# Three more panels of each channel mixer multiply a second pair of weight chunks with seven products

## The chip, the cores and the metric

The kernel runs on one core of one Trainium2 chip. The metric is the device time of a run in microseconds (us). Before the change it is 2210.26 us, the median of three runs (2210.10, 2210.26 and 2210.79). One more execution was taken by the hardware profiler; all views of the profile belong to it.

## The reference, cut to what matters

The model is a decoder trunk of two layers over 256 tokens of width 2048. Each layer has a mixer (gated linear attention in the first, forgetting attention in the second, both beside a cross-attention on 256 memory tokens) and then a channel mixer of hidden width 5632:

```
def conv_ffn(h, w_up, conv_w, conv_b, w_down):
    u = causal_dwconv(h @ w_up, conv_w, conv_b)
    a, val = split_cols(u, [FFN_HIDDEN, FFN_HIDDEN])
    return (jax.nn.silu(a) * val) @ w_down
```

The change touches only `h @ w_up`, a product of 256 x 2048 with 2048 x 11264 numbers, once in each layer. All data are 32-bit floats.

## The kernel before, in words

**Split numbers.** Each operand of a matrix product is split in a high part that TensorE takes as `fp32r` and a low part, the rest. One product of two split numbers is three matmuls: high by high, low by high, high by low. The weights come from memory in units of 128 partitions x 1024 numbers into a ring of five buffers `raw` (`split_unit`, load at L224). ScalarE (ACT in the profile) writes the high part `whi` (L234), VectorE (DVE) subtracts and writes the low part `wlo` (L235). `whi` and `wlo` are rings of five buffers each, so splitting can run at most a few units ahead of TensorE (PE). Both steps are scheduled with a raised priority (`AHEAD`).

**A panel.** `h @ w_up` is cut in eleven panels (`up_pair(j)`, j = 0, 4, ..., 40; panel number j // 4). A panel has 1024 columns, half for `a` and half for `val`, and its 2048 rows are 16 units, one for each chunk of 128 rows. The 256 tokens are two blocks and the columns two halves, so a unit needs four block products, each of three matmuls of 128 x 128 by 128 x 512: twelve matmuls.

**Seven products.** `pair_steps` can treat two neighbouring chunks together as a 2 x 2 block product, with seven products in place of eight (Strassen's scheme in Winograd's form): 21 matmuls instead of 24. It needs sums of the token blocks of the two chunks, made once for a layer (`input_sums`, into `usum`), and sums of the weights, made for each panel. So for a pair the weights go into two buffers `raw2` (L432, a ring of two; the loads are issued after the last load already issued), the raw values of three blocks are split as they are (L383, L384, first 512 columns and then 1024), four subtractions of 512 columns on VectorE form the sums in place (L438 to L441), and the two buffers are split once more (1024 columns each). The third split on ScalarE is issued after the last of these subtractions. The products p1, p5, p7 and p6 collect over all pairs of a panel in one set of four accumulators and p2, p3, p4 and x collect in the other; the two sets change places from panel to panel. After the last pair `early` combines the first set (L1503 to L1510); at the end of the panel `late` adds the second (L1514) and a transpose follows (L1465).

**Which panels.** Every panel takes the pair of chunks 6 and 7 that way (`SEVEN_UP`). Panels whose number stands in `MORE_IN` take chunks 11 and 12 as well (`SEVEN_MORE`). A panel with one pair runs six single units, the pair, and eight single units. A panel with two pairs runs the first pair after four single units, then three single units, the second pair, and five more. The `usum` of the second pair is made during the first panel, at its step 13 (L1524).

**What follows a panel.** Its two halves leave through GpSimd's (POOL's) DMA queue to DRAM and back, turned (L651, L656), and then need on ScalarE twelve scaled copies each (L1415) and an activation (L1428), and on VectorE two additions (L1422), one product (L1435) and a split (L529, L530). For four of the halves of a layer VectorE also makes token sums for the down projection (L477 to L480, L688, L689). These steps are put between the units of the next panels by `tick`: a step is let go 7 or 8 units after the panel's end, and each unit adds a credit of 1.45 (1.7 in panels with two pairs; none for a pair) that the steps use up; the two halves of a panel cost 20.4 together.

**Order in a layer.** Panels 0 to 4; two down projections of 16 units over the first 16 hidden chunks; panels 5 to 7; two of 12 units; panels 8 to 10; and the last four column groups of the down projection, which begin with a wide one that has a pair of its own. Each engine runs its instructions in one fixed order, made when the kernel is built, and loads of weights run in order on one queue (SP's).

Of the kernel before, what the change touches and what calls it, by code (L numbers as in the profile page):

```python
# [34 lines left out]
SEVEN_UP = (6,)  # L35
SEVEN_DOWN = {4: 0, 10: 1, 20: 0, 34: 1}
SEVEN_MORE = 11
MORE_IN = (2, 5, 6, 8, 9)
SCRATCH = 4096


# [106 lines left out]
def _trunk(ctx: ExitStack, tc: tile.TileContext, xt, xtok, memt, wp, wgu, gns, gfin, cnv, par, msk, out):  # L148
# [1246 lines left out]
    def ffn(l, nx, h, m, ys, zs, landing, then, pool, temps, last=None, spare=None):  # L1395
        with tc.tile_pool(name=f"ffn{l}", bufs=1) as fp:
# [60 lines left out]
            def turn(j, wait):  # L1457

                count[0] += 1
                slot = count[0] % 2  # L1460
                y, z = ys[slot], zs[slot]

                def evac(b, a):
                    with tc.high_priority(offset=AHEAD):
                        turned_last[0] = V.transpose(y[:, :, :, b, :], a.rearrange("p (k c i) -> p c k i", c=4, i=32))  # L1465
                    if b:
                        away = far_away(dram, flat(y), T, nc.gpsimd)
                        back = lambda: away(flat(z))
                        steps = [(0.5, lambda s=s, c=c, i=i: tap_of(j, s, c, i, slot)) for n in ((1, 2), (0,))
                                 for s in range(2) for c in range(2) for i in n]  # L1470
                        steps += [(1.0, lambda: add_tap(1)), (1.0, lambda: add_tap(2)), (0.5, silu),
                                  (1.0, lambda: gated(j, 0)), (0.7, lambda: gated(j, 1))]
                        returns.append((clock[0] + 3, slot, back, [(clock[0] + wait, *step) for step in steps]))

                return evac
# [18 lines left out]
            def up_pair(j):  # L1494

                count[2] += 1
                second = j // 4 in MORE_IN
                turns = [turn(j + 2 * h_, 7 if not h_ and j // 4 + 1 in MORE_IN else 8) for h_ in range(2)]
                u = {}

                def early(bank):
                    u.update({(b, h_): temps(2 * b + h_) for b in range(2) for h_ in range(2)})
                    S.activation(u[0, 1], bank["p1"], AF.Copy)  # L1503
                    S.activation(u[0, 0], bank["p1"], AF.Copy, scale=scale(0))
                    V.tensor_tensor(u[0, 1], bank["p6"], u[0, 1], ALU.add)
                    V.tensor_tensor(u[1, 0], bank["p7"], u[0, 1], ALU.add)
                    V.tensor_tensor(u[0, 1], bank["p5"], u[0, 1], ALU.add)
                    V.tensor_tensor(u[1, 1], bank["p5"], u[1, 0], ALU.add)
                    for b, h_ in ((0, 1), (1, 0), (1, 1)):
                        S.activation(u[b, h_], u[b, h_], AF.Copy, scale=scale(b))  # L1510

                def late(b, h_, a):
                    with tc.issue_after(turned_last[0].ins) if h_ and not b else nullcontext():
                        V.scalar_tensor_tensor(u[b, h_], a, scale(b), u[b, h_], ALU.mult, ALU.add)  # L1514
                    turns[h_](b, u[b, h_])

                return pair_steps(where["up", l, j], h, {k: up_sums[k] for k in (*SEVEN_UP, SEVEN_MORE)[: 1 + second]},
                                  count[2] % 2, pool, early, late, 2 * second)
# [8 lines left out]
            def drive(steps, share=1.45):  # L1527
                for k in steps:
                    tick(share if k >= 0 else 0.0)

            def drive_up(j):
                drive(up_pair(j), 1.7 if j // 4 in MORE_IN else 1.45)

# [266 lines left out]
```

## Time and profile before

| what | value |
|---|---|
| median of three runs | 2210.26 us |
| the profiled execution's own time | 2211.01 us |
| its span in the profile | 2209.2 us |
| PE busy | 2197.2 us, 10303 matmuls |
| DVE busy | 1804.7 us |
| ACT busy | 1426.7 us |
| first channel mixer, panels 0 to 10 | from 457 us to 1075 us of the span |
| second channel mixer, panels 0 to 10 | from 1494 us to 2113 us |

In the views, PE is TensorE, a name such as L413 is the line of the kernel at which the instruction was issued, and `x144` counts instructions. `acc`, `ps_o`, `ps_s` and `ps_t` are accumulators. `fvt` and `temp` are buffers for what a panel leaves, and `raw` stands for both `raw` and `raw2`, since instructions are named by the program's names without their numbers.

### The profile page before, as it was taken

How to read it: one execution, taken by the hardware profiler on the slowest of the kernel's cores; microseconds unless marked ns; L12 is line 12 of the kernel's file. 1: busy time of each engine (PE TensorE's matmuls, PEld its weight loads, DVE VectorE, ACT ScalarE, POOL GpSimd, SP SyncE). 2: the span in 40 equal slices, each digit the busy share in tenths (PEclk: the TensorE clock that was granted, in tenths of full speed). 3: DMA queues.
4: the chain of work that ended last, by engine and by line, in shares of the span. 5: the costliest groups of instructions: out<-in, count | busy, mean ns of one | idle time of the engine just before them, and what ended most of it. 6: DMA issues, size and time to landing. Idle time of an engine off the chain costs nothing.

```text
span 2209.2 us, 30105 instructions
## 1 busy us (share of the span) xinstructions
PE 2197.2 (99%) x10303; PEld 1849.1 (84%) x10303; DVE 1804.7 (82%) x2679; ACT 1426.7 (65%) x2268; POOL 137.2 (6%) x257
## 2 busy tenths in 40 slices
PE   9999999999999999999999999999999999999998
PEld 7888888888888888888888998888888888888886
DVE  7768976688998888889877669668898888888996
ACT  6655655556787568657865555455788657765774
POOL 0000000001100010001110000000100000100010
PEclk9999999999999999999999999999999999999999
DMA  9777677867778567666778767776677757676673
GB/s 367 253 223 220 192 209 225 256 219 249 235 248 267 189 212 248 229 232 221 247 252 259 227 201 244 228 240 231 227 239 236 254 184 247 228 266 206 223 271 131
DMA packets 166291, 515.42 MB, mean 233 GB/s; under 512 B 20780, under 2 KB 42552, under 8 KB 166136
## 3 DMA queue, kind: packets, MB, share of 16 engines
q1 hardware_dynamic: 149064, 460.99, 63.1%
q0 software_dynamic: 16496, 51.71, 7.4%
q8 instruction: 81, 1.33, 0.2%
q10 hardware_dynamic: 576, 0.79, 0.1%
q14 instruction: 74, 0.61, 0.1%
HBM read 469.62 MB, written 43.79 MB: 232 GB/s over the span
## 4 chain that ended last, share of the span: by engine, by line
PE 99%; DVE 0%; ACT 0%; issue 0%; DVEq 0%; ACTq 0%
PE acc L413 29%; PE acc L339 26%; PE ps_s L413 15%; PE ps_o L413 8%; PE ps_t L413 7%; PE acc L310 3%; PE acc L265 3%; PE ps_s L339 2%; PE acc L369 2%; PE acc L263 1%; PE ps_s L1036 0%; PE ps_o L702 0%; PE ps_s L702 0%; PE ps_s L1309 0%; PE ps_s L1082 0%; PE ps_o L1264 0%
## 5 line engine op out<-in xcount | busy, mean ns | idle before, releaser
L235 DVE TENSOR_TENSOR wlo<-raw,whi 128x1024 fp32r<-128x1024 f32 (+2 forms) x697 | 828.0, 1201 | 235.3 <-ACT whi L234 214.4
L234 ACT ACTIVATE whi<-raw 128x1024 fp32r<-128x1024 f32 (+2 forms) x697 | 717.6, 1046 | 356.1 <-PE acc L339 135.2
L339 PE MATMUL acc<-whi,B 128*128 128x512 f32 (+3 forms) x1248 | 290.9, 369 | 0.0
L383 ACT ACTIVATE whi<-raw 128x1024 fp32r<-128x1024 f32 (+1 forms) x160 | 151.9, 954 | 197.1 <-DVE raw L439 64.5
L339 PEld LDWEIGHTS acc<-whi,B 128*128 128x128 f32 x1248 | 226.8, 188 | 28.1
L384 DVE TENSOR_TENSOR wlo<-raw,whi 128x1024 fp32r<-128x1024 f32 (+1 forms) x160 | 173.4, 1085 | 25.9 <-ACT whi L383 23.5
L413 PE MATMUL acc<-whi,mix 128*128 128x512 f32 x750 | 191.9, 389 | 0.0
L413 PE MATMUL acc<-whi,B 128*128 128x512 f32 x728 | 188.4, 389 | 0.0
L413 PEld LDWEIGHTS acc<-whi,mix 128*128 128x128 f32 x750 | 140.8, 188 | 29.3
L413 PEld LDWEIGHTS acc<-whi,B 128*128 128x128 f32 x728 | 136.6, 188 | 28.4
L339 PE MATMUL acc<-wlo,B 128*128 128x512 f32 (+3 forms) x624 | 159.1, 369 | 0.0
L339 PEld LDWEIGHTS acc<-wlo,B 128*128 128x128 f32 x624 | 114.2, 188 | 14.6
L1415 ACT ACTIVATE tap<-yzu,cw 128x256 f32<-128x256 f32 x264 | 121.2, 534 | 2.6 <-DVE wlo L235 1.9
L1415 ACT ACTIVATE tap<-fvt,cw 128x256 f32<-128x256 f32 x264 | 121.2, 534 | 0.3 <-DMA fvt<-far 0.3
L1422 DVE TENSOR_TENSOR tap<-tap,tap 128x1024 f32<-128x1024 f32 x88 | 106.7, 1213 | 5.9 <-ACT tap L1415 5.9
L413 PE MATMUL acc<-wlo,mix 128*128 128x512 f32 x375 | 105.6, 389 | 0.0
L413 PE MATMUL ps_s<-whi,mix 128*128 128x512 f32 x382 | 105.1, 389 | 0.0
L413 PE MATMUL acc<-wlo,B 128*128 128x512 f32 x364 | 104.6, 389 | 0.0
L413 PE MATMUL ps_s<-whi,B 128*128 128x512 f32 x336 | 92.1, 389 | 0.0
L413 PEld LDWEIGHTS ps_s<-whi,mix 128*128 128x128 f32 x382 | 71.7, 188 | 14.9
L413 PEld LDWEIGHTS acc<-wlo,mix 128*128 128x128 f32 x375 | 70.4, 188 | 14.6
L413 PEld LDWEIGHTS acc<-wlo,B 128*128 128x128 f32 x364 | 68.3, 188 | 14.2
(502 smaller groups left out, 3890.2 us busy)
## 6 DMA issues: line engine op xcount, KB each, us to landing
raw<-wp SPq DMA_DIRECT2D x741, 512.0 KB, 4.7
fvt<-far POOLq DMA_DIRECT2D x100, 128.0 KB, 3.9
raw<-wp SPq DMA_DIRECT2D x32, 384.0 KB, 3.5
far<-yu POOLq DMA_DIRECT2D x22, 512.0 KB, 3.7
far<-yzu POOLq DMA_DIRECT2D x22, 512.0 KB, 4.3
yzu<-far POOLq DMA_DIRECT2D x88, 128.0 KB, 4.3
raw<-wp SPq DMA_DIRECT2D x24, 388.0 KB, 3.7
x<-xtok SPq DMA_DIRECT2D x8, 512.0 KB, 7.3
```

What stands on the lines that cost most here:

```text
L234: casts.append(S.activation(hi[:, s], raw[:, s], AF.Copy))
L235: lows.append(V.tensor_tensor(lo[:, s], raw[:, s], hi[:, s].bitcast(F32), ALU.subtract))
L263: mm = TE.matmul(acc[p][c][:, :T], w[:, s], both[:, 0, :], start=False, stop=end and j == 3)
L265: mm = TE.matmul(acc[p][c], w[:, s], both, start=u == j == 0, stop=end and j == 3)
L310: mm = TE.matmul(acc[b][:, :n], src[kcs[j] - base][:, part, b * P : (b + 1) * P], w, start=u == 0 and low == part == j == 0, stop=u == end ...
L339: mm = TE.matmul(acc[b][:, :n], src[kc - base][:, part, b * P : (b + 1) * P], ready[low][:, j * room : j * room + n], start=i == low == pa ...
L369: mm = TE.matmul(acc[b][:, :n], src[kc - base][:, part, b * P : (b + 1) * P], w, start=i == low == part == j == 0, stop=i == end and low = ...
L383: casts.append(S.activation(hi[:, :n], src, AF.Copy))
L384: lows.append(V.tensor_tensor(lo[:, :n], src, hi[:, :n].bitcast(F32), ALU.subtract))
L413: r = TE.matmul(bank[name], x, w, start=name not in begun, stop=last)
L1415: S.activation(by_run(taps[i][:, s, c, i:]), zs[slot][:, :, 2 * c + s], AF.Copy if i else AF.Identity, bias=0.0 if i else w[3], scale=w[2 ...
L1422: V.tensor_tensor(taps[0], taps[0], taps[n][:, :, :, :T], ALU.add)
```

## The change

`MORE_IN` names three panels more: 1, 7 and 10, that is the second, the eighth and the eleventh. Panels 1, 2, 5, 6, 7, 8, 9 and 10 then take the second pair, and panels 0, 3 and 4 do not. Nothing else is edited.

```
-MORE_IN = (2, 5, 6, 8, 9)
+MORE_IN = (1, 2, 5, 6, 7, 8, 9, 10)
```

Three places read it, all in `ffn`. In `up_pair`, `second` gives the panel the chunks 11 and 12 and moves its first pair two units earlier, and `turn` lets the steps of a panel's first half go after 7 units instead of 8 when the next panel is in `MORE_IN`; that is new for panels 0, 6 and 9. In `drive_up`, the credit of a unit in the three panels is 1.7 instead of 1.45.

```
second = j // 4 in MORE_IN
turns = [turn(j + 2 * h_, 7 if not h_ and j // 4 + 1 in MORE_IN else 8) for h_ in range(2)]
...
drive(up_pair(j), 1.7 if j // 4 in MORE_IN else 1.45)
```

## The prediction, before the result was known

> **What bounds the kernel now.** I read the page's head first, then one row of the chain of work that ended last, then the waits of TensorE (PE).
>
> ```profile
> span 2209.2 us, 30105 instructions
> ...
> PE 2197.2 (99%) x10303; PEld 1849.1 (84%) x10303; DVE 1804.7 (82%) x2679; ACT 1426.7 (65%) x2268; POOL 137.2 (6%) x257
> ```
>
> ```profile
> 883.65 32.64 PE acc L413 x144
> ```
>
> ```profile
> PE ps_t L413 <- ACT whi L383: 0.9, 1, 0.9
> ```
>
> ```profile
> 1514.08 0.74 PE L413 MATMUL ps_t<-whi,usum 128*128 128x512 f32 x2 [0.94 <-ACT whi L383]
> ```
>
> PE is busy for 99% of the span. In the chain, 144 matmuls of the mixer take 32.64 us, 226.7 ns for each, with nothing between them. The only wait of PE inside the two mixers long enough to be listed is 0.9 us, once, on the split of a pair (at 1514.08 us, in panel 0 of the second layer). So a matmul less is worth 226.7 ns, as long as the splits arrive in time. How near they are to being late is the question, and for that I cut the first mixer into panels (the windows run from the first matmul of one panel to that of the next).
>
> ```profile
> core 0: us, PE busy (x) PEld busy (x) DVE busy (x) ACT busy (x) POOL busy (x), PEclk, DMA share, GB/s
> 499.86:542.70 42.84, 42.84 (x190) 35.47 (x189) 35.03 (x41) 33.17 (x54) 5.47 (x10) 1.00 0.77 260
> 542.70:584.97 42.27, 42.27 (x188) 34.83 (x186) 38.98 (x45) 30.00 (x46) 5.49 (x10) 1.00 0.66 202
> 584.97:627.81 42.84, 42.84 (x191) 35.47 (x189) 39.03 (x52) 35.88 (x61) 5.50 (x10) 1.00 0.78 266
> 798.49:840.65 42.16, 42.16 (x188) 34.91 (x187) 37.56 (x45) 32.72 (x52) 5.54 (x10) 1.00 0.65 222
> 840.65:883.49 42.84, 42.84 (x191) 35.47 (x190) 36.47 (x47) 33.97 (x56) 5.52 (x10) 1.00 0.74 242
> 1032.41:1075.25 42.84, 42.84 (x191) 35.47 (x190) 36.50 (x47) 34.01 (x56) 5.49 (x10) 1.00 0.76 253
> 1075.25:1118.00 42.75, 42.46 (x188) 34.84 (x187) 41.53 (x51) 30.64 (x50) 5.50 (x10) 1.00 0.73 237
> ```
>
> These are panels 1, 2, 3, 6, 7 and 10 and the start of the last down projection. A panel with one pair (1, 3, 7, 10) takes 42.84 us, which is 189 matmuls of 226.7 ns, and one with two (6) takes 42.16 us, 186 matmuls. The kernel thus shows the gain of a second pair itself: 0.68 us. Panel 2 took 0.11 us more than 186 matmuls.
>
> **The change part by part.** *Removed:* three matmuls in each of six panels (three in each layer), 18 x 226.7 ns = **4.08 us** off PE's chain.
>
> By the Trainium skill ("TensorE: Matmul & The Clock Gate", Part 1) back-to-back matmuls of 512 columns start 215.7 ns apart with a warm clock. That would make 3.88 us; the row here has 226.7 ns, so the measured figure stands.
>
> *Added on VectorE and ScalarE.* A pair replaces two unit splits; their durations, over panels 1 to 10 of the first layer:
>
> ```profile
> L235 DVE TENSOR_TENSOR wlo<-raw,whi 128x1024 fp32r<-128x1024 f32 x178 | 213.2, 1217 | 43.9 <-ACT whi L234 40.8 <-PE ps_t L413 1.2
> L384 DVE TENSOR_TENSOR wlo<-raw,whi 128x1024 fp32r<-128x1024 f32 x54 | 65.8, 1219 | 9.2 <-ACT whi L383 8.3
> ...
> L441 DVE TENSOR_TENSOR raw<-raw 128x512 f32<-128x512 f32 x18 | 12.4, 691 | 0.5
> L440 DVE TENSOR_TENSOR raw<-raw,raw 128x512 f32<-128x512 f32 x18 | 12.4, 691 | 0.5
> L439 DVE TENSOR_TENSOR raw<-raw,raw 128x512 f32<-128x512 f32 x18 | 12.3, 684 | 0.2
> L384 DVE TENSOR_TENSOR wlo<-raw,whi 128x512 fp32r<-128x512 f32 x18 | 12.2, 680 | 2.4 <-ACT whi L383 2.4
> L438 DVE TENSOR_TENSOR raw<-raw 128x512 f32<-128x512 f32 x18 | 12.2, 680 | 0.3
> ```
>
> ```profile
> L234 ACT ACTIVATE whi<-raw 128x1024 fp32r<-128x1024 f32 x180 | 186.1, 1058 | 58.5 <-PE acc L413 21.9 <-PE ps_t L413 21.6 <-DMA raw<-wp 7.1
> ...
> L383 ACT ACTIVATE whi<-raw 128x1024 fp32r<-128x1024 f32 x54 | 57.2, 1061 | 73.7 <-DVE raw L439 32.4 <-PE acc L413 22.7 <-PE ps_t L413 8.6
> ...
> L383 ACT ACTIVATE whi<-raw 128x512 fp32r<-128x512 f32 x18 | 11.4, 631 | 16.5 <-PE ps_t L413 8.6 <-PE acc L413 6.2 <-DVE temp L1514 1.7
> ```
>
> VectorE: 680 + 3 x 1219 - 2 x 1217 = 1903 ns for the low parts and 680 + 684 + 691 + 691 = 2746 ns for the sums: **4.65 us more in each new panel**. ScalarE: 631 + 3 x 1061 - 2 x 1058 = **1.70 us more**. As PE also finishes 0.68 us earlier, VectorE has to find 5.33 us in each of these panels. Its idle time there is 42.84 - 35.03 = 7.81 us in panel 1, 6.37 us in panel 7 and 6.34 us in panel 10, so the total fits. Whether it fits at the right place I read from idle gaps (in brackets) and from splits and the matmuls that need them:
>
> ```profile
> 526.64 1.23 DVE L235 TENSOR_TENSOR wlo<-raw,whi 128x1024 fp32r<-128x1024 f32 x1 [1.12 <-ACT whi L234]
> ...
> 536.56 1.23 DVE L235 TENSOR_TENSOR wlo<-raw,whi 128x1024 fp32r<-128x1024 f32 x1 [1.28 <-ACT whi L234]
> ...
> 539.51 1.23 DVE L235 TENSOR_TENSOR wlo<-raw,whi 128x1024 fp32r<-128x1024 f32 x1 [1.05 <-ACT whi L234]
> ...
> 863.13 0.69 DVE L1505 TENSOR_TENSOR fvt<-acc,fvt 128x512 f32<-128x512 f32 x1 [2.25 <-PE acc L413]
> ...
> 882.33 0.75 DVE L1514 SCALAR_TENSOR_TENSOR fvt<-ps_o,ny,fvt 128x512 f32<-128x512 f32 x1 [4.09 <-PE ps_o L413]
> ...
> 1074.09 0.75 DVE L1514 SCALAR_TENSOR_TENSOR fvt<-acc,ny,fvt 128x512 f32<-128x512 f32 x1 [3.67 <-PE acc L413]
> ```
>
> ```profile
> 568.31 1.06 ACT L383 ACTIVATE whi<-raw 128x1024 fp32r<-128x1024 f32 x1 [0.39 <-PE acc L413]
> ...
> 822.03 1.06 ACT L383 ACTIVATE whi<-raw 128x1024 fp32r<-128x1024 f32 x1 [0.39 <-DVE raw L441]
> ```
>
> ```profile
> 569.45 0.71 PE L413 MATMUL ps_t<-whi,usum 128*128 128x512 f32 x2
> ...
> 825.23 0.61 PE L413 MATMUL ps_t<-whi,usum 128*128 128x512 f32 x2
> ```
>
> *Panels 7 and 10.* Before, VectorE runs ahead there until it stands idle at the panel's end, 4.09 and 3.67 us, waiting for the last accumulators; panel 7 has 2.25 us more at `early`. That covers 5.33 us in panel 7 (6.34) and all but 1.66 us in panel 10. Because it waits for PE at that point before and after, little lateness should pass on to what follows.
>
> *Panel 1.* Its late gaps are 1.12 + 1.28 + 1.05 = 3.45 us. The nearest case is panel 6: it too follows a panel that inherits no copies of a panel before it, and it has two pairs. There the last split of the second pair ends at 823.09 and is used at 825.23, **2.14 us to spare**, and PE never waits. I take panel 1 to be like panel 6: no wait.
>
> *Panels 2, 7 and 10 as the inheritors.* Panel 2 is the nearest case for a second pair under the inherited copies and additions. Its last split ends at 569.37 and is used at 569.45: **0.08 us to spare**, with 0.11 us lost. If panel 2 starts later by what panel 1 leaves over, there is nothing to take it from. Bounds for one panel: below, no wait (panel 6); above, all that no gap covers, 5.33 - 3.45 = 1.88 us (panel 1, paid in panel 2) or 1.66 us (panel 10). I take 0.15 us for each of the six, 0.9 us in all, near the 0.11 us of panel 2, since that panel already bears both loads that meet in the new ones, a second pair and inherited copies.
>
> *Moved:* the first pair comes two units earlier, and with it its two loads, in one queue with the other loads (SP's).
>
> ```profile
> SPq L432 <- DVE wlo L384: 62.9, 12, 10.2
> ```
>
> A pair's loads wait for the two `raw2` buffers, until the pair before has been split: twelve waits in the first mixer, up to 10.2 us, and the next units' loads stand behind them. A new second pair adds one such wait. The five `raw` buffers ahead cover it, as they do in panels 2 and 6; without that cover ScalarE waits for data as at L234 in the row above, 7.1 us in these panels. The bytes loaded are the same. POOL's transfers keep their step, three units after a panel. The copies of panels 0, 6 and 9 start a unit earlier for one half, and the credit of 12 units at 1.7 is 20.4 against 14 at 1.45, 20.3, so as many are let go in a panel. I take all this at nothing; if the load were late, the price is the wait of the next rival.
>
> A new wait stands in ScalarE's own order: the third split of a pair waits for VectorE's sums, 32.4 us in the L383 row, and the units' splits and the copies stand behind it. The Trainium skill speaks against the change here ("TensorE: Matmul & The Clock Gate", the engine queue depths under Part 1): the queues of ScalarE and VectorE are strict FIFO. By that rule the delay passes on whole; the trace agrees on the order, but panel 6 had spare time behind it.
>
> *Sum:* against the profiled execution, 2211.01 - 4.08 + 0.9 = 2207.8 us (its span 2209.2 becomes 2206.0). That execution was 0.75 us above the median of the runs, so for a median I say **2207.1 us**, 0.14% less. From no change a measurement of this kernel can tell about 0.2%, here 4.4 us, more than the whole sum without waits.
>
> **The rivals.**
>
> *The second pair comes late (slower).* The place is the second pair of panels 2, 7 and 10, behind the loads at L432. If the 1.88 us of panel 1 lands in panel 2, and in panels 7 and 10 token sums of the down projection and the copies stand between the pairs and cost 1.5 us each, a layer loses 1.88 + 3.0 = 4.9 us and gains 2.04; the time is 2210.3 + 2 x 2.9 = about **2216 us**. It decides from 0.68 us of waiting for each new pair. For it speaks the spare time of 0.08 us; against it the idle ends of panels 7 and 10.
>
> *VectorE is the bound, and PE's gain turns into waits.* Start of the down projection after panel 10: VectorE is busy 41.53 of 42.75 us. If the 1.66 us of panel 10 is paid there and 0.3 to 0.4 us in panel 2, the 2.04 us of a layer are gone: **2210.3 us**. Against it: panel 10 ends with VectorE waiting for PE.
>
> *All of it, and a stall goes.* If no wait is added and the 0.9 us in the second layer's panel 0 falls away because all orders are made anew, 2210.3 - 5.0 = **2205.3 us**. Nothing in panel 0 but the start of its copies is edited, so this is weak.
>
> **How the numbers follow.** Forecast (a gain of 1.5 to 4.2 us, 2206.1 to 2208.8): 0.58. VectorE the bound (2208.8 to 2212): 0.18. Late pairs (2212 to 2218): 0.16, and three quarters of that is over 2214.7, where 0.2% is reached. The stall that goes: 0.08. So faster by over 0.2% 0.08, slower 0.12, within 0.80. The range leaves out the weak case and most of the late pairs: 2205.6 to 2212.5.
>
> **What would show it.** Right: 10285 matmuls; panels 1, 7 and 10 at 42.16 us in both layers; VectorE's idle gaps at L1514 at the end of panels 7 and 10 shrunk to about nothing; PE's waits at L383 under 1.5 us in all. Wrong: waits of PE on `whi` or `wlo` of pairs of a microsecond or more in panels 2, 7 or 10 or in the wide down projection after panel 10, or panels that lie 0.68 us shorter and a total that does not follow.

## The result: slower by 0.8%, and the profile after

The changed kernel takes **2228.10 us** (median of 6 runs, 2227.57 to 2230.20) against 2210.51 us of the kernel before (median of 6 runs): 1.0082 times the time, 95% interval 1.0069 to 1.0095. The forecast was 2207.1 us, with a range of 2205.6 to 2212.5. The profiled execution took 2227.64 us. First the page's head and the waits of PE for splits (total us, times, longest us):

```profile
span 2225.9 us, 30152 instructions
...
PE 2199.3 (99%) x10285; PEld 1844.2 (83%) x10285; DVE 1827.6 (82%) x2715; ACT 1436.5 (65%) x2280; POOL 136.8 (6%) x257
```

```profile
PE acc L413 <- ACT whi L383: 5.8, 5, 1.5
PE ps_o L413 <- ACT whi L383: 4.7, 4, 1.9
PE ps_t L413 <- ACT whi L383: 3.6, 6, 1.3
```

The 18 matmuls are gone, and in place of one listed wait of 0.9 us PE waits 14.1 us in fifteen places for splits of pairs. Then panels 1, 2, 7 and 10 of the first mixer, each from its first matmul to that of the next panel:

```profile
core 0: us, PE busy (x) PEld busy (x) DVE busy (x) ACT busy (x) POOL busy (x), PEclk, DMA share, GB/s
499.99:542.15 42.16, 42.16 (x187) 34.92 (x186) 37.72 (x44) 32.89 (x51) 5.45 (x10) 1.00 0.67 233
542.15:585.49 43.34, 43.02 (x187) 34.69 (x186) 40.24 (x50) 32.87 (x53) 5.48 (x10) 1.00 0.64 224
841.17:887.16 45.99, 43.44 (x187) 34.53 (x186) 41.19 (x52) 33.09 (x53) 5.51 (x10) 1.00 0.60 206
1036.08:1083.60 47.52, 43.42 (x187) 34.52 (x186) 40.93 (x53) 32.41 (x51) 5.50 (x10) 1.00 0.62 201
```

All four have 186 matmuls, 42.16 us at 226.67 ns. Panel 1 takes just that. Panel 2 takes 1.18 us more, panel 7 3.83 us and panel 10 5.36 us. I call this excess the loss of a panel; in the second mixer, counted in the same way, it is 1.19, 4.16 and 4.51 us. Panels 3 to 6, 8 and 9 lose nothing in either. The six losses are 20.2 us; 4.08 us of matmuls are saved; what is left, 16.1 us, is nearly the whole difference of the two profiled spans, 16.7 us. The losses are larger than the listed waits (5.4 against 4.1 us in panel 10): idle time is counted from the modelled end of the matmul before, 0.39 us after its start, and the two matmuls behind a wait take 0.73 us where two others take 0.62.

Where it goes in panel 10: the timeline of SP's queue, ScalarE and PE (start us, us; in brackets the idle time before and what ended it).

```profile
1050.01 1.67 SPq L432 DMA_DIRECT2D raw<-wp  x2
...
1057.37 0.63 ACT L383 ACTIVATE whi<-raw 128x512 fp32r<-128x512 f32 x1 [4.51 <-DMA raw<-wp]
1057.90 0.61 ACT L688 ACTIVATE dsum<-cv 128x512 fp32r<-128x512 f32 x1
1058.42 4.77 ACT L1415 ACTIVATE tap<-fvt,cw 128x256 f32<-128x256 f32 x11
1063.10 1.99 ACT L383 ACTIVATE whi<-raw 128x1024 fp32r<-128x1024 f32 x2
1066.96 1.06 ACT L383 ACTIVATE whi<-raw 128x1024 fp32r<-128x1024 f32 x1 [1.87 <-DVE raw L441]
...
1058.05 0.72 PE L413 MATMUL ps_o<-whi,B 128*128 128x512 f32 x2 [1.31 <-ACT whi L383]
1064.19 0.73 PE L413 MATMUL acc<-whi,B 128*128 128x512 f32 x2 [1.53 <-ACT whi L383]
1068.07 0.73 PE L413 MATMUL ps_t<-whi,usum 128*128 128x512 f32 x2 [1.27 <-ACT whi L383]
```

The second pair's two loads are issued 13.9 us into the panel. ScalarE comes to the pair's first split and stands idle for 4.51 us until the first load has landed, and the eleven scaled copies of panel 9 stand behind that split. They then run, 4.77 us, ahead of the second and third splits. PE waits three times. How long the loads took (KB each, median us from issue to landing), in panels 10 and 7, and in panel 10 what GpSimd's queue sent at the same time, the turned copies of the panel before (`fvt<-far`, L656):

```profile
raw<-wp SPq DMA_DIRECT2D x2, 512.0 KB, 7.8
fvt<-far POOLq DMA_DIRECT2D x4, 128.0 KB, 6.7
...
raw<-wp SPq DMA_DIRECT2D x2, 512.0 KB, 6.7
```

And VectorE, which the prediction took for the cover, in panels 7 and 10 before and after the point at which it is about done with the first pair (us, DVE busy, PEclk, DMA share, GB/s):

```profile
841.17:854.70 13.53, 13.50 (x22) 1.00 0.54 209
854.70:869.00 14.30, 9.66 (x13) 1.00 0.79 252
1036.08:1049.60 13.52, 13.52 (x21) 1.00 0.55 203
1049.60:1064.00 14.40, 8.12 (x12) 1.00 0.86 250
```

It is busy without a gap for 13.5 us, and then stands idle 4.6 and 6.3 us in the very stretch in which PE waits.

**The timetable that counts.** The second pair comes after 7 units and a pair, 105 matmuls, 23.8 us into the panel. Its products p1 to p3 are nine matmuls, so the third split is needed at 25.8 us; as it takes 1.06 us, it must begin by **24.8 us**. In panel 10 it is the second of the two at 1063.10 and begins near 1064.1, 28.0 us into the panel. In the trace it follows the second of the four subtractions (L439), and only the fourth split follows the last (L441). The fourth split is needed after 118 matmuls, 26.7 us into the panel; in panel 10 it ends at 1068.02, 31.9 us into it. Those 5.2 us are nearly the whole loss of the panel. The first of the three waits, which ends 22.0 us into the panel, comes before the pair's place because two matmuls of p1 stand 16 places ahead of it in PE's fixed order. The runs below are read against this.

### The profile page after: what moved, and what is told of

It reads as the page before. It is cut to its first block, busy times and chain, and to the rows that moved or that the text cites. A ratio compares the mean times of both kernels' runs of the same rounds, so it can differ in the third digit from the quotient of the medians.

```text
span 2225.9 us, 30152 instructions
## 1 busy us (share of the span) xinstructions
PE 2199.3 (99%) x10285; PEld 1844.2 (83%) x10285; DVE 1827.6 (82%) x2715; ACT 1436.5 (65%) x2280; POOL 136.8 (6%) x257
## 5 line engine op out<-in xcount | busy, mean ns | idle before, releaser
L235 DVE TENSOR_TENSOR wlo<-raw,whi 128x1024 fp32r<-128x1024 f32 (+2 forms) x685 | 812.3, 1200 | 218.7 <-ACT whi L234 201.4
L234 ACT ACTIVATE whi<-raw 128x1024 fp32r<-128x1024 f32 (+2 forms) x685 | 703.7, 1045 | 341.2 <-PE acc L339 136.3
L383 ACT ACTIVATE whi<-raw 128x1024 fp32r<-128x1024 f32 (+1 forms) x184 | 173.8, 951 | 192.8 <-DVE raw L439 70.6
L384 DVE TENSOR_TENSOR wlo<-raw,whi 128x1024 fp32r<-128x1024 f32 (+1 forms) x184 | 198.9, 1084 | 54.2 <-ACT whi L383 51.5
L1422 DVE TENSOR_TENSOR tap<-tap,tap 128x1024 f32<-128x1024 f32 x88 | 106.7, 1212 | 5.3 <-ACT tap L1415 5.3
L413 PEld LDWEIGHTS acc<-wlo,mix 128*128 128x128 f32 x373 | 70.0, 188 | 14.5
```

The lines of the kernel that those rows point to most:

```text
L234: casts.append(S.activation(hi[:, s], raw[:, s], AF.Copy))
L235: lows.append(V.tensor_tensor(lo[:, s], raw[:, s], hi[:, s].bitcast(F32), ALU.subtract))
L383: casts.append(S.activation(hi[:, :n], src, AF.Copy))
L384: lows.append(V.tensor_tensor(lo[:, :n], src, hi[:, :n].bitcast(F32), ALU.subtract))
L413: r = TE.matmul(bank[name], x, w, start=name not in begun, stop=last)
L1422: V.tensor_tensor(taps[0], taps[0], taps[n][:, :, :, :T], ALU.add)
```

## The experiments

The theory formed from the traces: panels 2, 7 and 10 lose because the second pair's splits come late, through late or slow loads (they wait for the two `raw2` buffers, so for the first pair's last low part) and through ScalarE's copies. The rivals: VectorE as a whole is too full; the token sums (the prediction's own late-pair rival). A loss per panel is given as first / second mixer; it belongs to the profiled execution. In brackets behind a time stand its ratio to the kernel before, measured with it, and the 95% interval. All diffs are shortened, and against the changed kernel unless something else is said.

**1 to 3. Each new panel alone** (against the kernel before).

```
-MORE_IN = (2, 5, 6, 8, 9)
+MORE_IN = (1, 2, 5, 6, 8, 9)      # run 1
+MORE_IN = (2, 5, 6, 7, 8, 9)      # run 2
+MORE_IN = (2, 5, 6, 8, 9, 10)     # run 3
```

> The kernel before with panel 1 alone given the second pair. Theory A (late data: in panels 7 and 10 the loads of the second pair land 7 to 8 us after their issue and ScalarE's fixed order puts ten or more copies between the pair's first and second split): panel 1 itself gains 0.68 us as in the trace after, panel 2 loses 1.1 us, so 2 x 0.4 = about 1 us slower than before, 2211 to 2212 us. Theory B (VectorE has too much to do): the three panels of a layer add the same 4.65 us each, so about a third of the whole loss, 6 us slower. Theory C (token sums of the down projection stand between the pairs): none stand in panel 1, so a gain of 1.4 us.

> The kernel before with panel 7 alone given the second pair. Theory A: the loss of panel 7 in the trace after, 3.15 us in the first layer and 3.48 us in the second, and nothing elsewhere, 6.6 us slower than before, about 2217 us. Theory B: a third of the loss, 6 us slower. Theory C: about half of the loss, 7 to 8 us slower.

> The kernel before with panel 10 alone given the second pair. Theory A: 4.68 and 3.83 us from panel 10 and some 1 us from the wide down projection behind it, 8.5 to 9.7 us slower than before, 2219 to 2220 us. Theory B: a third of the loss, 6 us. Theory C: about half of it, 7 to 8 us.

Panel 1 alone: 2211.99 us (ratio 1.0003, 0.9993 to 1.0012); it gains its own 0.68 us and panel 2 loses 1.23 / 1.93. Panel 7 alone: 2217.18 us (1.0030, 1.0019 to 1.0041), loss 4.03 / 4.61. Panel 10 alone: 2218.22 us (1.0033, 1.0020 to 1.0045), 5.40 / 2.99. Over the 2210.76 us of the kernel before in these runs that makes 1.2 + 6.4 + 7.5 = 15.1 us of the 17.6: the three panels are nearly independent, and each loses in its own place.

**4. The token sums away.** Pairs 20 and 34 of the down projection take eight products, so their sums are not made; PE gets 2.7 us more.

```
-SEVEN_DOWN = {4: 0, 10: 1, 20: 0, 34: 1}
+SEVEN_DOWN = {4: 0, 10: 1}
```

> The changed kernel without the seven products, and so without the token sums, for the pairs of hidden chunks 20 and 34: VectorE makes no token sums in panels 7 and 10, and the second and the third part of the down projection take three matmuls more each (2 x 2 x 0.68 = 2.7 us in all). What is computed stays the same. Theory C (token sums between the two pairs make the waits): panels 7 and 10 lose their waits, about 2228 - 15 + 2.7 = 2216 us. Theory A: the loads of the second pair can be issued at most 1.1 us earlier (four sums of 0.28 us), and the waits shrink by that at most: 2225 to 2231 us.

2227.12 us (1.0076, 1.0061 to 1.0091); panels 7 and 10 lose 3.57 / 4.16 and 5.19 / 5.17, 18.1 us where the changed kernel loses 17.9. VectorE is busy for 13.46 and 13.47 of the first 13.50 us of the two panels: other work took the room. Its total fell by some 39 us without an effect on these losses, so neither the token sums nor its load as such make them. (The time stays about the same although PE has 2.7 us more to do; what makes up for that lies outside these panels.)

**5. ScalarE's order.** The second pair's first split is issued behind the last copy already let go, so that ScalarE copies while the load is under way.

```
-    w1 = split_more(ra[:, :512], 512)
+    w1 = split_more(ra[:, :512], 512, copies if ahead and done else ())   # issued after copies[-1]
```

> The changed kernel, with ScalarE's first split of a second pair issued after the last copy already let go, so that the copies stand ahead of the pair and not between its first and second split. Work, loads and VectorE's instructions stay. Theory A: in panels 7 and 10 the second split starts when its data land (23 to 24 us after the panel's start instead of 25.4 to 27.0), and the waits of PE on the second and the fourth split, about 1.3 to 1.9 us and 1.3 us in each of four places, go down to nothing or little: 8 to 12 us faster than the changed kernel, 2216 to 2220 us; a wait on the first split stays. Theories B and C: no change, 2227 to 2229 us.

2223.22 us (1.0056, 1.0041 to 1.0071): 4.9 us of the loss went, not the 8 to 12 expected. Panels 7 and 10 still lose 2.51 / 3.95 and 2.43 / 3.00, as the second load still lands late (8.1 us after its issue in panel 10) and three splits hang on it.

**6 to 8. The second pair later.** Chunks 12 and 13, and 13 and 14, in place of 11 and 12; and the latter in the kernel before, as a control.

```
-SEVEN_MORE = 11
+SEVEN_MORE = 12      # run 6
+SEVEN_MORE = 13      # runs 7 and 8
```

> The changed kernel with chunks 12 and 13 instead of 11 and 12 as the second pair, so that it runs one unit (2.72 us) later in all eight panels that have it. Same matmuls, same VectorE and ScalarE work in all. Theory A, as it now stands (the second pair's weights can't be loaded until the first pair's two buffers are free, 13.9 and 15.3 to 15.7 us into panels 2, 7 and 10 because VectorE has work of the panel before in between, land 20 to 21 and 23 to 24 us in, and the pair's splits, with the copies, come 1 to 4 us after PE could start on them): each wait shrinks by up to 2.7 us, about 10 to 13 us faster than the changed kernel, 2215 to 2218 us. Theory B (VectorE has too much to do in these panels): the same work must be done in the same panels, no change, 2227 to 2229 us.

> The changed kernel with chunks 13 and 14 as the second pair, two units (5.44 us) later. Theory A: the splits are done before PE needs them, no waits are left in panels 2, 7 and 10, and the saving of 4.08 us shows: 2205 to 2210 us. Theory B: 2227 us or more, since less of the panel is left behind the second pair to catch up in. A rival of its own: only three units are left after the second pair, and the combining of its accumulators then comes so late that the next panel waits for them: 2210 to 2220 us, with waits at the start of panels.

> The kernel before with chunks 13 and 14 as the second pair in its five panels: the control for the run with the changed kernel. Theory A: nothing waits there but panel 2 (0.1 us), so 2210 to 2211 us. If the later pair itself costs (accumulators free too late), it shows here as waits at the start of panels.

2223.23 us (1.0060, 1.0044 to 1.0077), then 2238.70 us (1.0138, 1.0117 to 1.0160); the control 2210.56 us (1.0001, 0.9992 to 1.0010). Run 6 gained 4.9 us, not the 10 to 13 expected: panels 7 and 10 lose 2.68 / 2.18 and 3.75 / 1.97, but panel 2 now loses 4.25 / 3.04, half of it at its first pair. The expectation for run 7 fell. With two units more the second pair was in time, but the waits went to the *first* pair of the next panel, two units nearer now: in the profile, of an execution of 2248.21 us, panel 2 lost 3.91 / 4.69, panel 7 4.92 / 3.29, panel 10 3.02 / 2.99, and the down projection behind panel 7 1.46 / 6.81. What is put between the pairs inside a panel is taken from the distance across its end.

**9 and 10. Buffers.** One buffer goes from `raw` to `raw2` (4 and 3 in place of 5 and 2), in the changed kernel and in the one before.

```
-raw = rear.tile([P, NUNIT], F32, name="raw", tag="raw", bufs=5)
+raw = rear.tile([P, NUNIT], F32, name="raw", tag="raw", bufs=4)
-... tag="raw2", bufs=2)
+... tag="raw2", bufs=3)
```

> The changed kernel with three raw2 buffers instead of two and four raw buffers instead of five (there is no room for both). The first load of a second pair no longer waits for the first pair, and the second waits for its third split instead of its fourth, 1.3 to 1.7 us earlier. Theory A: the first split comes in time, the second and fourth 1.5 to 2 us earlier; panels 7 and 10 lose 2 us less each, 2218 to 2223 us, if the shorter raw ring costs nothing (the control says). Theory B: no gain, 2227 us or more.

> The kernel before with three raw2 and four raw buffers: the control for the run above. Where the loads have 4.7 us to land and a unit takes 2.72 us, four buffers should do: 2210 to 2212 us. If it is slower, the shorter ring costs that in the run above as well.

2230.11 us (1.0087, 1.0072 to 1.0102) and 2213.36 us (1.0012, 1.0002 to 1.0021). The shorter ring costs 2.5 us by itself. The pair's first load then came early, but the second, on which three of the four splits hang, was still issued 14.2 us into panel 7 and landed 6.9 us later. Panels 7 and 10 lost 2.27 / 2.66 and 2.14 / 2.42, 9.5 us in place of 17.9, while the time did not fall: what they gained was lost elsewhere, 2.5 us of it to the shorter ring. Three buffers beside five were not tried.

**11 to 13. The first pair back in its old place.** In panels 7 and 10 both pairs come two units later (run 11); the same with the second pair on chunks 12 and 13 and without panel 1 (run 12); of the new panels only 7 (run 13).

```
-count[2] % 2, pool, early, late, 2 * second)
+count[2] % 2, pool, early, late, 2 * (second and j // 4 not in (7, 10)))
 # runs 12 and 13 also: SEVEN_MORE = 12, MORE_IN = (2, 5, 6, 7, 8, 9, 10) and (2, 5, 6, 7, 8, 9)
```

> The changed kernel, with the two pairs of panels 7 and 10 alone run two units later (first pair after six single units, as in the kernel before, second pair after three more). Work and the distance between the two pairs stay. Theory A, in its present form (in the first 13.5 us of panels 7 and 10 VectorE is busy without a gap with work of the panel before, so the first pair is done late, its two buffers come free late, the second pair's weights land late, and VectorE then stands idle for 4.6 to 6.3 us while PE runs dry): with the first pair two units later VectorE has caught up, as it had in the kernel before, where its last split was 3.3 to 3.5 us ahead; panels 7 and 10 lose 0 to 1 us each instead of 3.8 to 5.4, 2210 to 2214 us. Theory B (VectorE has more work than PE in these panels): the same work, no change, 2226 to 2229 us.

> As the run with the later pairs in panels 7 and 10, with chunks 12 and 13 as the second pair in all panels that have one (one more single unit between the pairs) and panel 1 left with one pair, since panel 2 paid 1.1 us in each layer for it. Twelve matmuls fewer than the kernel before, 2.7 us. Theory A: next to no waits are added, 2207.8 to 2210 us, faster than both kernels. Theory B: VectorE's extra 4.65 us in panels 7 and 10 still cost several us each, 2216 us or more. A rival: with two units left after the second pair, its accumulators are combined too late for what follows, waits at the start of the next stage.

> Only panel 7 of the three is new, its pairs at steps 6 and 12, and the second pair is chunks 12 and 13 in every panel. Six matmuls fewer than before (1.36 us). From the run with panel 10 as well: no wait in panel 2, 7 or 8, and a wait of 1.3 and 0.2 us in the pair of the down projection after panel 7, so about 2210.8 - 1.4 + 1.5 = 2211 us. If the second pair of panel 10 was the sole cause of the rest there, 2209.5 to 2211.5 us; if the 2 us that the parts behind panel 10 lost have another cause, 2213 to 2216 us.

2217.46 us (1.0036, 1.0023 to 1.0049), 2216.28 us (1.0024, 1.0015 to 1.0034) and 2212.63 us (1.0012, 1.0003 to 1.0021). In run 11 panels 7 and 10 lose 0.00 / 2.79 and 1.76 / 2.52, under half of the changed kernel's, in a profiled execution of 2222.51 us, 5 us above the median, in which panel 2 loses 2.59 / 1.81; so the earlier place of the pairs is a part of the cause. In run 12 panels 2, 7 and 10 all run without loss, yet the time is 5.5 us over the kernel before: waits turned up in the next pairs, 1.3 / 0.3 us in the down projection behind panel 7 and about 2 us behind panel 10 in each mixer. Run 13 has only the first of these, 0.59 / 0.94 us, and 0.51 us in panel 7 of the second mixer. The misses are of one kind: I expected what was removed in a place to stay removed.

**14 to 16. VectorE's work or the traffic.** What stood against each other now: VectorE is full before the first pair is split, so the loads go out late; or the loads land slowly because the turned copies of the panel before (L656) are in flight. Run 14 drops the additions at L1422, run 15 three of four turned copies, run 16 both; so these three kernels leave out a part of the computation.

```
 # run 14, in add_tap
-    V.tensor_tensor(taps[0], taps[0], taps[n][:, :, :, :T], ALU.add)
+    return
 # run 15, in far_away and turn
-    for c in range(4):
+    for c in range(parts):
-    back = lambda: away(flat(z))
+    back = lambda: away(flat(z), 1)
```

> The changed kernel without the two additions of each half at L1422 (the three taps of the convolution are no longer summed, only the first is used): four instructions of 1.21 us, 4.8 us of VectorE in each panel, half of them in the first 13.5 us of panels 7 and 10, before the first pair's sums. Theory that VectorE's queue before the first pair makes the second pair's loads late: the first pair's last low part ends 2.4 us sooner, the loads start sooner by as much, and 2.4 us of the 4 to 5.4 us go in each of panels 7 and 10, and the 1.2 us in panel 2: 2214 to 2219 us. Rival, that slow landing of these loads beside the turned copies in POOL's queue sets the end: they land as late, 2226 to 2229 us. Rival, that VectorE's order is only made anew and other work takes the room, as it did without the token sums: no change, 2226 to 2229 us.

> The changed kernel with one of the four turned copies of each half from DRAM (L656) in place of four (three quarters of the values that the convolution reads are zeros set once): the traffic that is in flight from 11 to 24 us of panels 7 and 10 beside the second pair's loads shrinks to a quarter. Theory that the landing of these loads beside that traffic costs 2 to 3 us in each late pair (6.1 to 8.4 us there, 4.7 to 4.9 us in the middle of all): they land in about 5 us and 2 to 3 us go in each of panels 7 and 10: 2216 to 2221 us. Theory that VectorE alone makes the pair late: the loads start as late, the rest waits for ScalarE's copies all the same: 2225 to 2229 us.

> Both at once: no additions at L1422 and one turned copy of four. If late issue (VectorE) and slow landing (the queues) add up, 4.5 to 5.5 us go in each of panels 7 and 10 and 1.2 us in panel 2, which is all of the loss: 2206 to 2210 us. If only one of the two counts, the time is that of the run with that one alone.

2214.25 us (1.0018, 1.0008 to 1.0027), 2215.31 us (1.0021, 1.0012 to 1.0030), 2214.34 us (1.0019, 1.0009 to 1.0029): each alone takes about three quarters of the loss away and both together no more. The traces show why these are one effect. Run 15, panel 10 (columns as in the views of panels above), its loads, and ScalarE there:

```profile
1033.90:1077.40 43.50, 42.80 (x187) 34.78 (x186) 40.40 (x53) 32.24 (x51) 2.25 (x4) 1.00 0.54 190
```

```profile
raw<-wp SPq DMA_DIRECT2D x2, 512.0 KB, 4.3
```

```profile
1050.17 4.78 ACT L1417 ACTIVATE tap<-fvt,cw 128x256 f32<-128x256 f32 x11
...
1059.25 1.06 ACT L383 ACTIVATE whi<-raw 128x1024 fp32r<-128x1024 f32 x1 [2.31 <-DVE raw L439]
```

VectorE is as full and the loads go out only 0.4 us sooner, 13.5 us into the panel, but they land in 4.3 us in place of 7.8. The copies now run while they are under way, ScalarE's 4.51 us of idle time are gone, and the third split begins 25.3 us into the panel, 0.5 us late, and the fourth behind it; 1.3 us are still lost there. In run 14 the loads went out no sooner (13.9 us into panel 10), against my expectation, but they too landed in 4.3 us. Dropping the additions had let VectorE turn the panel before sooner, so that GpSimd sent the first half's copies early. First the changed kernel's panel 10 (starts at 1036.08), then run 14's (1033.5):

```profile
1047.05 2.21 POOL L656 DMA_DIRECT2D fvt<-far  x4
```

```profile
1039.91 2.18 POOL L656 DMA_DIRECT2D fvt<-far  x4 [2.98 <-issue]
```

11.0 us into the panel in the one, 6.4 us in the other. So run 14 is a run on the traffic too.

**17. The copies behind the second pair.** With the whole computation kept, the turned copies after panels 1, 6 and 9 and their steps are let go later.

```
-returns.append((clock[0] + 3, slot, back, [(clock[0] + wait, *step) for step in steps]))
+returns.append((clock[0] + (6 if late_ else 3), slot, back,
+                [(clock[0] + (12 if late_ else wait), *step) for step in steps]))
```

> The changed kernel, all of its computation, with the turned copies of what panels 1, 6 and 9 leave moved from 3 to 6 units after the panel and their steps (scaled copies, additions, product) from 7 or 8 to 12 units, so that in panels 2, 7 and 10 they come behind the second pair. Theory that the landing of the second pair's loads beside the turned copies, and ScalarE's copies between that pair's first two splits, make the loss: the loads land in 4 to 5 us, the second split stands behind no copies, and the 4 to 5.4 us of panels 7 and 10 and the 1.2 us of panel 2 go: 2206 to 2210 us, less if nothing follows, more if the later steps then crowd the down projections. Theory that VectorE's full queue before the first pair sets the end: the loads are issued as late and at least 1.5 us stay in each of these panels: 2212 us or more.

2225.29 us (1.0065, 1.0048 to 1.0082): a miss, and the trace says why. Only ScalarE's copies had moved. GpSimd waited for nothing new, so its turned copies still went out 11 us into the panel, and the loads in panel 7 still took 7.0 us.

Panels 7 and 10 lose 3.17 / 3.62 and 2.93 / 4.73. With the copies out of the way and the loads still slow, 14.5 of the 17.9 us are left in these four panels.

**18. The turned copies behind the landing.** A one-column copy on GpSimd that reads the pair's second load holds them back; the steps come at 13 units.

```
+gate = pool.tile([P, 1], F32, name="gate", tag="gate", bufs=1)     # after the two loads, in panels 2, 7, 10
+touched[0] = nc.gpsimd.tensor_copy(gate, rb[:, :1])
 # and the turned copies, at 11 units: with tc.issue_after(touched[0].ins): back()
```

> The changed kernel, all of its computation, with the turned copies after panels 1, 6 and 9 tied behind the landing of the second pair's loads in panels 2, 7 and 10 (a one-column copy on GpSimd reads the second of them, and the turned copies come behind it in GpSimd's order), and their steps 13 units after the panel. In the run before this one the turned copies still went out from 11 us of the panel on, because nothing made them wait; there the loads landed in 6.3 to 8.6 us. If their landing beside that traffic is what is left: the loads land in 4 to 5 us, no more than 1.5 us of loss stays in panel 7 and in panel 10 and 1.2 us or less in panel 2; 2206 to 2212 us. If something else slows those loads, they land in 6 us or more as before, and the time is 2222 to 2228 us. A third way: the steps that come later crowd the down projections behind panels 2, 7 and 10, with waits there and a time between.

**2212.58 us** (median of 11; ratio 1.0010, 1.0001 to 1.0020), 15.5 us less than the change. Panel 10, its loads (4.1 us there and in panel 7, with no turned copies on the way), and its second and third split on ScalarE:

```profile
1031.90:1074.30 42.40, 42.40 (x187) 34.80 (x186) 39.80 (x51) 28.99 (x44) 5.72 (x11) 1.00 0.68 222
```

```profile
raw<-wp SPq DMA_DIRECT2D x2, 512.0 KB, 4.1
```

```profile
1051.92 1.06 ACT L383 ACTIVATE whi<-raw 128x1024 fp32r<-128x1024 f32 x1 [1.43 <-DMA raw<-wp]
1055.68 1.07 ACT L383 ACTIVATE whi<-raw 128x1024 fp32r<-128x1024 f32 x1 [2.70 <-PE acc L415]
```

The third split begins 23.8 us into the panel, a microsecond ahead of its deadline, and the losses of panels 2, 7 and 10 are 0.31 / 0.41, 0.44 / 0.38 and 0.28 / 0.92 us: 2.0 us are left of 17.9 in panels 7 and 10. The loads still go out as late as in the changed kernel, 14.0 us into panel 7.

With runs 15 and 17 this shows the cause: loads that are issued late and land slowly beside the turned copies, and ScalarE's copies in between. Run 18 also moves the additions and the product of the panel before on VectorE and so does not part the copies from them; but VectorE had time to spare there. That late issue and slow landing both count is seen by comparing the changed kernel's panels 6 and 2, whose loads take:

```profile
raw<-wp SPq DMA_DIRECT2D x2, 512.0 KB, 6.2
...
raw<-wp SPq DMA_DIRECT2D x2, 512.0 KB, 5.1
```

In panel 6 they go out 9.6 us into the panel, beside eight turned copies, and nothing is lost. In panel 2 they go out at 13.9 us, as in panels 7 and 10, but land sooner, and 1.18 us are lost in place of 3.83 and 5.36.

Run 18 is still no gain. Of the 4.08 us, 2.7 go in these panels, and other waits of PE have grown:

```profile
PE acc L339 <- ACT whi L234: 1.5, 1, 1.5
PE acc L369 <- ACT whi L234: 1.5, 1, 1.5
```

These two stand in the last part of the down projections, behind panel 10, at lines that no run edits; in the profile of before they are 0.3 us each. The 2.4 us that they grew by and the 2.7 us are more than the 4.08 us saved. Why they grew is open. No version that was run beats the kernel before.

## Why the prediction was wrong

*Removed.* Right: 10285 matmuls, and panel 1 at 42.16 us.

*Added.* Right in size: VectorE is busy 41.19 us in panel 7 and 40.93 us in panel 10, 4.72 and 4.43 us more than before, where 4.65 was forecast. (Over the whole span it is 22.9 us more, 3.8 for each of the six panels, and ScalarE 9.8 us more, 1.6 for each, where 1.70 was forecast.)

*"Panels 7 and 10 ... That covers 5.33 us".* **This step failed.** I set the added work against VectorE's idle time of the whole panel. But that idle time lay at 22.5 us (at `early`) and at the panel's end, and the second pair needs its third split to begin by 24.8 us. Nothing idle stood ahead of the first pair's last low part, on which the second pair's loads wait: they go out 14.0 and 13.9 us into panels 7 and 10, where the model case, panel 6, has 9.6. The gaps at L1514 did shrink to nothing, as the prediction said they would, and proved nothing: time that an engine has free after the deadline covers no work before it.

*"Moved ... I take all this at nothing".* **The other half of the same failure.** "The five `raw` buffers ahead cover it" holds for the units behind a pair in SP's queue, not for the pair's own loads, which have two buffers. I also wrote that POOL's transfers keep their step. In time they do not. In panel 10 before, which starts at 1032.41, the eight turned copies went out 14.3 to 22.6 us into the panel:

```profile
1046.73 2.19 POOL L656 DMA_DIRECT2D fvt<-far  x4 [5.85 <-issue]
...
1052.87 2.19 POOL L656 DMA_DIRECT2D fvt<-far  x4 [3.40 <-ACT whi L234]
```

In the changed kernel they go out 11.0 to 16.0 us into it, on both sides of the pair's loads at 13.9. Panel 2 before had shown it coming: the same pair of loads, issued 12.2 us into the panel, took

```profile
raw<-wp SPq DMA_DIRECT2D x2, 512.0 KB, 5.4
```

and its last split was ready 0.08 us ahead of its matmul. In panels 7 and 10 the loads went out 1.8 and 1.7 us later and took 6.7 and 7.8 us. Why VectorE gets to the first pair's low parts that much later there isn't settled. It has additions, token sums and a product of the panel before ahead of them, which panel 6 has not; but without the token sums (run 4) and without the additions (run 14) the loads went out no sooner.

*"Panel 1 like panel 6".* Right for panel 1. *"Panel 2 ... 0.15 us".* Mis-sized: 1.18 / 1.19 us, and 1.23 / 1.93 with panel 1 alone. The upper bound of 1.88 us was the better guide, since nothing was to spare.

*ScalarE's own order.* The rule that the prediction weighed, strict FIFO queues (the Trainium skill, "TensorE: Matmul & The Clock Gate", Part 1), was set aside because panel 6 had spare time. It held: one split that waits 4.51 us for a load pushed the eleven copies behind it, and through them the next two splits, later. Run 18 shows the difference: there a split waits 1.43 us for a load with no copies behind it, and the panel loses 0.28 us.

*The rivals.* The late pair was the right one, at the right place, with the wrong price and half of the cause: token sums and copies between the pairs at 1.5 us each. The token sums count for nothing in these panels (run 4); the copies count, and the loads, whose lateness it named without their slow landing, more; 3.8 to 5.4 us a panel, not 1.5. So 2216 us was too low as well. VectorE as the bound fell in run 4 and by its 4.6 and 6.3 us of idle time while PE waits. The stall in the second mixer's panel 0 shrank (0.94 us listed before, 0.36 after) but did not go.

## What to carry to other kernels

Idle time covers added work only if it stands ahead of the added work's deadline in the engine's fixed order, so write the timetable of the new operation (load issued, landed, split, summed, split again, needed) before adding up free microseconds. For a load that waits on a buffer, take the issue time from what frees the buffer and the landing time from loads that share the same stretch with other queues, not from the median of all. A wait that is removed is worth what it cost only when the next deadline behind it has spare time: in runs 6, 7, 11, 12 and 13 waits turned up at the next pairs.

## What was not expected of the hardware

*After a wait of 1.8 us TensorE ran at half its rate, and after others as long it did not.* In run 7 PE waited for the first pair of panel 2. First PE's timeline, then its windows (us, PE busy, PEclk, DMA share, GB/s):

```profile
556.93 1.43 PE L413 MATMUL ps_s<-whi,usum 128*128 128x512 f32 x4 [1.81 <-ACT whi L383]
...
559.42 1.06 PE L413 MATMUL acc<-whi,B 128*128 128x512 f32 x2
560.28 1.02 PE L413 MATMUL ps_s<-wlo,usum 128*128 128x512 f32 x2
```

```profile
558.60:562.00 3.40, 3.40 (x10) 0.63 0.80 212
562.00:565.40 3.40, 3.40 (x16) 1.00 1.03 277
```

After it, a stretch with a granted clock of 0.63 runs 10 matmuls where the next runs 16; from 559.42 to 560.28 two matmuls take 430 ns each in place of 227. The loss goes on behind the wait. That agrees with the 426.7 ns that the Trainium skill gives for a cold array ("TensorE: Matmul & The Clock Gate", Part 1); it ties the drop to an idle window of about 3.4 us, and here it came after a wait of 1.8 us. The length of one wait does not decide it. Behind another wait of 1.81 us in run 7 (before 1056.28 us) the clock stayed at 1.00, and so it did in the changed kernel behind its longest wait, where two matmuls took the usual 0.73 us:

```profile
1913.98 0.73 PE L413 MATMUL ps_o<-whi,A 128*128 128x512 f32 x2 [1.92 <-ACT whi L383]
```

In run 9 the clock fell behind a wait of 1.23 us (before 1120.58 us):

```profile
1122.60:1126.00 3.40, 3.40 (x9) 0.52 0.69 245
```

On what else it depends no run here shows.

*The same 512 KB load takes 4.1 us or 7.8 us* (median of a pair's two loads) by what the other queue has in flight: 4.1 us with nothing of it, 4.3 us beside turned copies cut to a quarter, 7.8 us with four turned copies of 128 KB sent in the 3 us before and four in the 2 us behind it.
